# Hybrid attention and S5 block: PSUM copies moved to ScalarE, and three stretches reordered

## The chip, the core and the metric

The kernel runs on one core of a Trainium2 chip. The metric is the time of one execution on the device in microseconds (us). The engines are called PE (TensorE, matrix products and transposes, results in PSUM), DVE (VectorE), ACT (ScalarE), POOL (GpSimd) and SP (SyncE, which issues most DMAs). PE, DVE and ACT each work through a queue of their own in order, and wait on semaphores for one another.

## What is computed

One layer of a decoder trunk over 512 tokens of width 1024, all in float32. Two sub-layers, each with RMS norms and a modulation from a condition vector:

```python
h = rms_norm(x) * (1 + sc1) + sh1
z = h @ w_in                      # feeds three causal mixers
y_gla = gated_linear_attention(...)   # 4 heads; chunk state + in-chunk scores
y_ml  = mlstm(short_convolution(...)) # 4 heads
y_s5  = s5_state_space(...)           # 32 groups, complex diagonal states
merged = gate0*(y_gla@proj_gla) + gate1*(y_ml@proj_ml) + gate2*(y_s5@proj_s5)
x = x + (1 + gt1) * rms_norm(merged @ w_out)
h = rms_norm(x) * (1 + sc2) + sh2
x = x + (1 + gt2) * rms_norm((silu(h@w_gate) * (h@w_up)) @ w_down)
```

## The kernel before

**Products in three passes.** To get float32 accuracy, each operand of a large product is split into a high and a low half (`split`, line 234): ACT casts the high half (line 229), DVE subtracts to get the low half (line 220). A product is then three matmuls (`passes`, line 421: high by high, high by low, low by high). So each weight tile of 128x1024 costs ACT one cast and DVE one subtraction, and PE's pass with the low half waits for DVE.

**Who fixes the order.** In most of the kernel the instructions are written in program order and a planner sorts each engine's queue by its own idea of costs and priorities; the trace shows the sorted order, with later work often ahead of earlier work. The start (`head`) and the stretch from the output projection to the first part of the feed-forward network (`region`, from line 1627) are under `manual_schedule`: there PE, DVE and ACT follow the written order.

**Fillers.** Large projections of h (the gates, the attention's values, the S5 inputs and so on) are jobs that `fill(n)` and `FL.until(...)` place between the steps of the mixers, so that PE has products to do while DVE and ACT work on a mixer. Each job ends with a function that takes the result out of PSUM: `ev_conv` (first step of the short convolution), `ev_su` (S5 input, written in reversed order), `ev_gv` and others.

**Attention (lines 910 to 1206).** After the first projection sweep, q, k and the decay logits are copied out of PSUM (`qT`, `kT`, `ga`, `ii`, `lf`), a log-sigmoid chain on ACT gives the decays, `level` builds the scores `ST` (DVE-heavy, 14 calls), `kdT` holds the transposed decayed keys. Then, for each pair of heads `p`, the states `Sg` of the first three tiles of 128 tokens follow one another. After that comes, tile by tile, the output `og[t]`: tile 0 needs no state, tiles 1 to 3 need that of the tile before. Each output is scaled by the diagonal and squared for the norm; `rstd` is a chain of twelve small DVE steps; then 16 scalings by the norm and the gate `gr` (tile by tile, inside it head by head), and `to_fm` transposes 16 blocks of 128x128, four to a head, from which head by head the halves for the next product are made. PSUM banks for all these small products come from a pool of four (`ax_bank`).

**S5 (lines 1210 to 1331).** `params(b)` builds tables by outer products on DVE (`outer`), with a small product `ks` taken out of PSUM; `states(b)` and `outputs(b)` follow.

**Output projection (lines 1584 to 1683).** `half(t, h)` is the projection of token tile t, half h of the columns (24 matmuls). `gated`, `normed`, `x1_out`, `second` are the norms and the residual on ACT and DVE, the last giving `xn`; `to_h2(t)` transposes `xn` (8 transposes) and splits the result into `h2`. `S.ahead(ffn0_i[j], 0)` makes the halves of a weight tile, hi(j) and lo(j). `slab0(t)` is the first slab of the feed-forward product of tile t (24 matmuls, two k-steps to a weight tile).

Of the kernel before, what the change touches and what calls it, by code (L numbers as in the profile page):

```python
# [8 lines left out]
AF = mybir.ActivationFunctionType  # L9
OP = mybir.AluOpType  # L10
# [174 lines left out]
def _emit(tc, nc, ctx, ExitStack, A, out, act, dve, pool, pe, sp):  # L185
# [23 lines left out]
    def slot(name="s", dt=F32, tag="s"):  # L209
        return pools[tag].tile([128, 512], dt, tag=tag, name=name)  # L210
# [4 lines left out]
    def ax_bank(name="ax"):  # L215
        return axp.tile([128, 512], F32, tag="ax", name=name)
# [5 lines left out]
    def ts(e, o, a, s1, s2, op0, op1=OP.bypass):  # L222
        e.tensor_scalar(out=o, in0=a, scalar1=s1, scalar2=s2, op0=op0, op1=op1)

    def stt(o, a, s, b, op0, op1):
        dve.scalar_tensor_tensor(out=o, in0=a, scalar=s, in1=b, op0=op0, op1=op1)  # L226
# [4 lines left out]
    def cp(o, i, e=dve):  # L231
        e.tensor_copy(out=o, in_=i)
# [12 lines left out]
    def P(name, i=None, n=1, rows=slice(0, 128)):  # L245
        o, w = _PV[name]
        return pv[rows, o:o + w] if i is None else pv[rows, o + i:o + i + n]
# [107 lines left out]
    S = Stream()  # L355
# [296 lines left out]
    def ev_conv(f):  # L652
        def e(ps):
            u = slot("conv", tag="v")
            w = lambda j: P("conv_w", f * 4 + j)
            ts(dve, u, ps, w(3), P("conv_b", f), OP.mult, OP.add)
            for j in range(3):
                d = 3 - j
                stt(u[:, d:512], ps[:, 0:512 - d], w(j), u[:, d:512], OP.mult, OP.add)
            af(u, u, AF.Silu)  # L660
            conv[f] = u
        return e
# [3 lines left out]
    def ev_su(f):  # L666
        def e(ps):
            u = slot("su")
            cp(u.rearrange("p (a n) -> p a n", a=8)[:, ::-1], ps.rearrange("p (n a) -> p a n", a=8))
            sp.dma_start(out=su_d[f].rearrange("a p n -> p a n"), in_=u.rearrange("p (a n) -> p a n", a=8))  # L670
            U[f] = upool.tile([128, 512], F32, tag="U", name="U")
            sp.dma_start(out=U[f], in_=su_d[f].rearrange("a (c g) n -> (a c) (g n)", g=8))
        return e
# [242 lines left out]
    for p in range(2):  # L916
        qT[p], kT[p] = slot("gq"), slot("gk")
        af(qT[p], sweep_ps[p], AF.Copy, scale=0.125)
        cp(kT[p], sweep_ps[2 + p])
    ts(dve, ii[0:4], ii[0:4], P("i_b", rows=slice(0, 4)), None, OP.add)  # L920
    fill(1)
    cum = {}
# [208 lines left out]
    for p in range(2):  # L1131
        cv = cum[p].rearrange("p (t i) -> p t i", t=4)
        kd = slot("kd")
        kdv = kd.rearrange("p (t i) -> p t i", t=4)
        tt(dve, kdv[:, 0:3], cv[:, 0:3, 127:128].broadcast_to([128, 3, 128]), cv[:, 0:3], OP.subtract)
        af(kd[:, 0:384], kd[:, 0:384], AF.Exp, scale=1.0 / 16)
        tt(dve, kd[:, 0:384], kd[:, 0:384], kT[p][:, 0:384], OP.mult)
        ecum[p] = slot("ecum", tag="y")
        af(ecum[p], cum[p], AF.Exp, scale=1.0 / 16)
        qE[p] = slot("qE", tag="y")  # L1140
        tt(dve, qE[p], ecum[p], qT[p], OP.mult)
        ps = ax_bank()
        for t in range(3):
            pe.transpose(out=ps[:, t * 128:(t + 1) * 128], in_=kd[:, t * 128:(t + 1) * 128], identity=ident)
        kdT[p] = slot("kdT", tag="y")
        cp(kdT[p][:, 0:384], ps[:, 0:384])
    FL.until("gv")
    fill(2)
    for p in range(2):
        Sg[p] = slot("Sg", tag="y")  # L1150
        for t in range(3):
            ps = ax_bank()
            mm(ps[:, 0:256], lhsT=kdT[p][:, t * 128:(t + 1) * 128], rhs=gv[t][:, p * 256:(p + 1) * 256],
               start=True, stop=True)
            for h in range(2):
                r = slice(64 * h, 64 * h + 64)
                o = Sg[p][r, t * 128:(t + 1) * 128]
                if t == 0:
                    cp(o, ps[r, h * 128:(h + 1) * 128])
                else:  # L1160
                    stt(o, Sg[p][r, (t - 1) * 128:t * 128], ecum[p][r, t * 128 + 127:t * 128 + 128],
                        ps[r, h * 128:(h + 1) * 128], OP.mult, OP.add)
        fill(1)
    og = {}
    ssg, rg = st3[:, 16:32], st3[:, 32:48]
    for t in range(4):
        ps = [ax_bank(), ax_bank()]

        for h in range(4 if t else 0):
            p, hh = h // 2, h % 2  # L1170
            r = slice(64 * hh, 64 * hh + 64)
            mm(ps[hh][:, p * 128:(p + 1) * 128], lhsT=qE[p][r, t * 128:(t + 1) * 128],
               rhs=Sg[p][r, (t - 1) * 128:t * 128], start=(p == 0), stop=False)
        for h in range(4):
            p, hh = h // 2, h % 2
            a = (t % 2) * 2 + hh
            mm(ps[hh][:, p * 128:(p + 1) * 128], lhsT=ST[p, t // 2][:, a * 128:(a + 1) * 128],
               rhs=gv[t][:, h * 128:(h + 1) * 128], start=(t == 0 and p == 0), stop=(p == 1))
        og[t] = slot("og")
        for h in range(4):  # L1180
            sl = slice(h * 128, (h + 1) * 128)
            stt(og[t][:, sl], gv[t][:, sl], dg[:, t * 4 + h:t * 4 + h + 1],
                ps[h % 2][:, (h // 2) * 128:(h // 2 + 1) * 128], OP.mult, OP.add)
            junk = slot("junk")
            af(junk[:, 0:128], og[t][:, sl], AF.Square, accum_out=ssg[:, t * 4 + h:t * 4 + h + 1])
        fill(1)
    rstd(rg, ssg, 16, 128.0)
    FL.until("gr")
    for t in range(4):
        for h in range(4):  # L1190
            sl = slice(h * 128, (h + 1) * 128)
            stt(og[t][:, sl], og[t][:, sl], rg[:, t * 4 + h:t * 4 + h + 1], gr[t][:, sl], OP.mult, OP.mult)
    fill(5)
# [43 lines left out]
    def params(b):  # L1237
        pr = slice(4 * b, 4 * b + 4)
        CA[b] = big("CA")
        outer(CA[b], s5c[:, 0], s5c[:, 1], 0, pr, -1)  # L1240
        wp = big("wp")
        outer(wp, bb[:, 0], bb[:, 1], 1, pr, 1)
        bs = slot("bs")
        bv = bs[:, 0:256].rearrange("p (g c) -> p g c", c=32)
        pool.memset(bs[:, 0:256], 0.0)
        b2 = bv[:, :, 0:16].rearrange("p (a g) c -> p a g c", g=2)
        for g, r, q in ((0, even, odd), (1, odd, even)):
            cp(b2[r, :, g], bb[r, 0, pr])
            cp(b2[q, :, g], bb[r, 1, pr])
        fill(1)  # L1250
        kp = ax_bank()
        for g in range(8):
            q = (g % 4) * 32
            mm(kp[q:q + 32, (g // 4) * 128:(g // 4 + 1) * 128], lhsT=bv[:, g], rhs=CA[b][:, g * 128:(g + 1) * 128],
               start=True, stop=True, tile_position=(0, q))
        ks = slot("ks")
        cp(ks[:, 0:256], kp[:, 0:256])
        for j in range(2):
            stt(ks[:, j * 128:j * 128 + 16], C("dmask"), P("s5_d", 2 * b + j), ks[:, j * 128:j * 128 + 16],
                OP.mult, OP.add)  # L1260
        for q in range(4):
            sp.dma_start(out=kd_d.rearrange("(j q) c x -> q c j x", q=4)[q, :, 2 * b:2 * b + 2, 128:256],
                          in_=ks[q * 32:q * 32 + 16, 0:256].rearrange("p (j x) -> p j x", j=2))
        WT[b] = big("WT")
        for h in range(2):
            ps = ax_bank()
            for g in range(4):
                o = (h * 4 + g) * 128
                pe.transpose(out=ps[:, g * 128:(g + 1) * 128], in_=wp[:, o:o + 128], identity=ident)
            (lambda o, i: af(o, i, AF.Copy))(WT[b][:, h * 512:(h + 1) * 512], ps)  # L1270
        Mt[b] = big("M")
        for a in range(8):
            sp.dma_start(out=Mt[b][a * 16:(a + 1) * 16].rearrange("p (g x) -> p g x", g=8),
                         in_=kd_d[8 * b:8 * b + 8, :, 16 + 16 * a:144 + 16 * a].rearrange("g c x -> c g x"))
        fill(2)
# [278 lines left out]
    def normed(t):  # L1554

        r = root_inv(col(t))
        for h in range(2):
            stt(yg[t][h], yg[t][h], r, xre[t][h], OP.mult, OP.add)
# [80 lines left out]
    gated(2, yp, wslot)  # L1639
    S.ahead(ffn0_i[0], 0)  # L1640
    half(3, 0)
    normed(2)
    to_h2(0)
    S.ahead(ffn0_i[1], 0)
    x1_out(2)
    S.ahead(ffn0_i[2], 0)
    to_h2(1)
    S.ahead(ffn0_i[3], 0)
    half(3, 1)
    second(2)  # L1650
    x_tile(3, wslot, A["x"], sp)
    gated(3, yp, wslot)
    slab0(0)
    to_h2(2)
    normed(3)
    x1_out(3)
    slab0(1)
    second(3)
    slab0(2, range(4))
    slab0_g(0)  # L1660
# [85 lines left out]
```

## Time and profile before

| | |
|---|---|
| median of 3 runs | 912.28 us (910.48 to 912.75) |
| the profiled execution | 910.4 us, span of its instructions 908.6 us |
| PE busy in the span | 98% |
| DVE busy | 63% |
| ACT busy | 36% |
| mean granted TensorE clock | 0.989 |

A row of a timeline gives the start from the beginning of the span, the duration, the engine, the line, the operation, the program's names (output<-inputs), the shapes and how many instructions are merged into it; in brackets stands how long the engine sat idle before it and what ended that. L220, L226, L229 and L232 are helpers (`tt`, `stt`, `af`, `cp`), so names tell more than lines. Durations overlap a little: the distance from one start to the next is what an instruction costs its engine. The profile models the end of a matmul, so PE reads as busy when its matmuls follow closely, whatever paces them.

### The profile page before, as it was taken

Reading aid. Unit: us, or ns where it says so; the run is one execution under the profiler, and the core shown is the slowest. Engines: PE = TensorE matmul, PEld = TensorE weight load, DVE = VectorE, ACT = ScalarE, POOL = GpSimd, SP = SyncE. Lnnn points to the kernel's source line nnn. Section 1 sums busy time; section 2 is a strip of 40 time slices with the busy share of each in tenths; the row PEclk is TensorE's granted clock in tenths of the full one; section 3 lists DMA queues with packets and bytes.
Section 4 is the critical chain, followed back from the end, with each engine's and each line's share of the span. In section 5 each row is a group of like instructions: output and inputs, shape, how many; then the busy total and the mean of one; then the engine's idle time right before and its main releaser. Section 6 shows DMA issues by size and latency. Waiting matters only on the chain.

```text
span 908.6 us, 11582 instructions
## 1 busy us (share of the span) xinstructions
PE 888.7 (98%) x4334; PEld 723.1 (80%) x4334; DVE 575.7 (63%) x1144; ACT 331.0 (36%) x512; POOL 24.9 (3%) x68
## 2 busy tenths in 40 slices
PE   9999999999989999999999989999999999999997
PEld 7667887878878878788888868888888888888885
DVE  6748999979879884966679497544433333322215
ACT  4339323431442462722334444333222332211113
POOL 2010000000000000010000000000000000000000
PEclk7999999999999999999999999999999999999999
DMA  9661341233443442345456533533333323322303
GB/s 364 251 193 47 116 128 58 82 125 111 154 139 108 121 116 93 131 127 172 153 175 226 199 140 117 185 116 117 118 126 130 113 93 116 115 93 97 113 1 139
DMA packets 52193, 120.79 MB, mean 133 GB/s; under 512 B 13797, under 2 KB 19429, under 8 KB 52137
## 3 DMA queue, kind: packets, MB, share of 16 engines
q1 hardware_dynamic: 49944, 115.92, 38.0%
q0 software_dynamic: 1040, 2.38, 1.1%
q10 hardware_dynamic: 1152, 1.75, 0.5%
q8 instruction: 34, 0.56, 0.3%
q14 instruction: 23, 0.18, 0.1%
HBM read 113.21 MB, written 6.82 MB: 132 GB/s over the span
## 4 chain that ended last, share of the span: by engine, by line
PE 77%; DVE 17%; issue 2%; ACT 2%; DMA 1%; SPq 0%; DVEq 0%; ACTq 0%
PE mm L422 16%; PE mm L423 16%; PE mm L424 16%; PE y L1527 5%; PE y L1526 5%; PE y L1528 5%; DVE lo L220 3%; PE mm L455 2%; PE mm L454 2%; PE mm L456 2%; DVE ST L1111 1%; DVE Qp L220 1%; DVE o L220 1%; DVE D L220 1%; PE ax L1318 1%
## 5 line engine op out<-in xcount | busy, mean ns | idle before, releaser
L229 ACT ACTIVATE hi<-raw 128x1024 fp32r<-128x1024 f32 (+2 forms) x157 | 151.9, 971 | 382.2 <-PE mm L423 156.2
L220 DVE TENSOR_TENSOR lo<-raw,hi 128x1024 fp32r<-128x1024 f32 (+2 forms) x157 | 174.6, 1114 | 155.6 <-ACT hi L229 155.0
L424 PE MATMUL mm<-h2hi,lo 128*128 128x512 f32 x320 | 124.6, 389 | 0.0
L423 PE MATMUL mm<-h2lo,hi 128*128 128x512 f32 x320 | 124.6, 389 | 0.0
L422 PE MATMUL mm<-h2hi,hi 128*128 128x512 f32 x320 | 124.5, 389 | 0.0
L424 PE MATMUL mm<-hT,lo 128*128 128x512 f32 x280 | 110.7, 395 | 3.1 <-DVE lo L220 3.1
L422 PE MATMUL mm<-hT,hi 128*128 128x512 f32 x280 | 112.3, 401 | 0.2 <-ACT hT L229 0.2
L423 PE MATMUL mm<-hT,hi 128*128 128x512 f32 x280 | 111.0, 396 | 0.4 <-DVE hT L226 0.4
L422 PEld LDWEIGHTS mm<-h2hi,hi 128*128 128x128 f32 x320 | 60.1, 188 | 12.5
L424 PEld LDWEIGHTS mm<-h2hi,lo 128*128 128x128 f32 x320 | 60.1, 188 | 12.4
L423 PEld LDWEIGHTS mm<-h2lo,hi 128*128 128x128 f32 x320 | 60.1, 188 | 12.3
L1528 PE MATMUL y<-hi,g 128*128 128x512 f32 x176 | 68.5, 389 | 0.0
L1527 PE MATMUL y<-lo,g 128*128 128x512 f32 x176 | 68.5, 389 | 0.0
L1526 PE MATMUL y<-hi,g 128*128 128x512 f32 x176 | 68.3, 389 | 0.0
L220 DVE TENSOR_TENSOR sg<-sg,mm 128x512 f32<-128x512 f32 x36 | 24.7, 685 | 64.8 <-PE mm L424 64.7
L422 PEld LDWEIGHTS mm<-hT,hi 128*128 128x128 f32 x280 | 53.2, 190 | 15.7 <-issue 4.0
L424 PEld LDWEIGHTS mm<-hT,lo 128*128 128x128 f32 x280 | 53.2, 190 | 14.6 <-DVE lo L220 3.5
L423 PEld LDWEIGHTS mm<-hT,hi 128*128 128x128 f32 x280 | 53.1, 190 | 11.9 <-DVE hT L226 1.2
L226 DVE SCALAR_TENSOR_TENSOR gacc<-raw,cact,gacc 128x512 f32<-128x512 f32 x56 | 41.9, 748 | 21.9 <-DMA raw<-ada 21.3
L455 PE MATMUL mm<-lo,hT 128*128 128x512 f32 x128 | 50.5, 394 | 0.4 <-DVE lo L220 0.4
L454 PE MATMUL mm<-hi,hT 128*128 128x512 f32 x128 | 49.8, 399 | 0.0
L456 PE MATMUL mm<-hi,hT 128*128 128x512 f32 x128 | 49.7, 391 | 0.0
(311 smaller groups left out, 1393.9 us busy)
## 6 DMA issues: line engine op xcount, KB each, us to landing
raw<-ada SPq DMA_DIRECT2D x48, 512.0 KB, 3.5
raw<-ffn SPq DMA_DIRECT2D x44, 512.0 KB, 3.3
raw<-wzg SPq DMA_DIRECT2D x24, 512.0 KB, 3.2
raw<-ffo SPq DMA_DIRECT2D x22, 512.0 KB, 3.3
raw<-wpr SPq DMA_DIRECT2D x24, 256.0 KB, 2.7
raw<-wout SPq DMA_DIRECT2D x8, 512.0 KB, 4.3
raw<-sweep SPq DMA_DIRECT2D x8, 384.0 KB, 8.5
xT<-xT SPq DMA_DIRECT2D x4, 512.0 KB, 5.6
```

Source lines behind the costliest of these rows:

```text
L220: e.tensor_tensor(out=o, in0=a, in1=b, op=op)
L226: dve.scalar_tensor_tensor(out=o, in0=a, scalar=s, in1=b, op0=op0, op1=op1)
L229: act.activation(out=o, in_=i, func=f, **kw)
L422: mm(ps, lhsT=whi, rhs=xhi, start=first, stop=False)
L423: mm(ps, lhsT=whi, rhs=xlo, start=False, stop=False)
L424: mm(ps, lhsT=wlo, rhs=xhi, start=False, stop=last)
L454: mm(ps[t], lhsT=xh[:, tk], rhs=hi[:, sl], start=(k == 0), stop=False)
L455: mm(ps[t], lhsT=xh[:, tk], rhs=lo[:, sl], start=False, stop=False)
L456: mm(ps[t], lhsT=xl[:, tk], rhs=hi[:, sl], start=False, stop=(k == 7))
L1526: mm(ps, lhsT=xhi, rhs=whi[:, sl], start=first, stop=False)
L1527: mm(ps, lhsT=xhi, rhs=wlo[:, sl], start=False, stop=False)
L1528: mm(ps, lhsT=xlo, rhs=whi[:, sl], start=False, stop=last)
```

## The change

Sixteen copies or first steps out of PSUM move from DVE (`cp`, `ts`) to ACT (`af`): the first step of the convolution, the S5 input, `kT`, `kdT` and `ks`. In the attention, the body of the output loop becomes `gla_out(t)`; tile 0's outputs are written ahead of the states, and the 16 scalings go head by head, inside that tile by tile. In the output projection, `half(3, 1)` moves between the two transposes of tiles 0 and 1, the second norm of tile 2 moves behind the gating of tile 3, and tile 2's transposes move behind tile 3's norm and between the halves of `slab0(1)`.

```diff
-            ts(dve, u, ps, w(3), P("conv_b", f), OP.mult, OP.add)
+            af(u, ps, AF.Identity, scale=w(3), bias=P("conv_b", f))
...
-            cp(u.rearrange("p (a n) -> p a n", a=8)[:, ::-1], ps.rearrange("p (n a) -> p a n", a=8))
+            af(u.rearrange("p (a n) -> p a n", a=8)[:, ::-1], ps.rearrange("p (n a) -> p a n", a=8), AF.Copy)
...
-        cp(kT[p], sweep_ps[2 + p])
+        af(kT[p], sweep_ps[2 + p], AF.Copy)
...
-        cp(kdT[p][:, 0:384], ps[:, 0:384])
+        af(kdT[p][:, 0:384], ps[:, 0:384], AF.Copy)
     FL.until("gv")
     fill(2)
-    for p in range(2):
-        Sg[p] = slot("Sg", tag="y")
...
     og = {}
     ssg, rg = st3[:, 16:32], st3[:, 32:48]
-    for t in range(4):
+    def gla_out(t):
         ps = [ax_bank(), ax_bank()]
...
         fill(1)
+
+    gla_out(0)
+    for p in range(2):
+        Sg[p] = slot("Sg", tag="y")
...
+        fill(1)
+    for t in range(1, 4):
+        gla_out(t)
     rstd(rg, ssg, 16, 128.0)
     FL.until("gr")
-    for t in range(4):
-        for h in range(4):
+    for h in range(4):
+        for t in range(4):
             sl = slice(h * 128, (h + 1) * 128)
             stt(og[t][:, sl], og[t][:, sl], rg[:, t * 4 + h:t * 4 + h + 1], gr[t][:, sl], OP.mult, OP.mult)
...
-        cp(ks[:, 0:256], kp[:, 0:256])
+        af(ks[:, 0:256], kp[:, 0:256], AF.Copy)
...
     half(3, 0)
-    normed(2)
     to_h2(0)
     S.ahead(ffn0_i[1], 0)
+    half(3, 1)
+    normed(2)
+    S.ahead(ffn0_i[2], 0)
     x1_out(2)
-    S.ahead(ffn0_i[2], 0)
+    S.ahead(ffn0_i[3], 0)
     to_h2(1)
-    S.ahead(ffn0_i[3], 0)
-    half(3, 1)
-    second(2)
     x_tile(3, wslot, A["x"], sp)
     gated(3, yp, wslot)
+    second(2)
     slab0(0)
-    to_h2(2)
     normed(3)
     x1_out(3)
-    slab0(1)
+    slab0(1, range(4))
+    to_h2(2)
+    slab0(1, range(4, 8))
     second(3)
```

## Rows read from the trace of the kernel before

**Rows 1.** The page, part 1: busy us, share of the span, instructions of each engine.

```profile
PE 888.7 (98%) x4334; PEld 723.1 (80%) x4334; DVE 575.7 (63%) x1144; ACT 331.0 (36%) x512; POOL 24.9 (3%) x68
```

**Rows 2.** The waits of PE: engine, line, releaser: us in total, times, longest.

```profile
PE mm L424 <- DVE lo L220: 3.1, 1, 3.1
PE ax L1580 <- DVE xn L220: 1.9, 3, 0.7
PE ax L1200 <- DVE og L226: 1.6, 1, 1.6
...
PE ax L1177 <- DVE Sg L226: 1.1, 1, 1.1
```

**Rows 3.** Windows: stretch, length, busy us of PE, PEld, DVE, ACT, POOL, clock, DMA.

```profile
66.00:77.00 11.00, 10.93 (x45) 7.75 (x44) 8.20 (x13) 8.89 (x10) 0.00 (x0) 1.00 0.18 51
77.00:160.00 83.00, 81.31 (x440) 68.34 (x438) 81.59 (x228) 34.92 (x54) 0.00 (x0) 1.00 0.28 89
...
168.00:190.00 22.00, 20.36 (x88) 15.76 (x86) 21.68 (x50) 5.88 (x11) 0.31 (x1) 0.92 0.25 83
190.00:233.00 43.00, 43.00 (x293) 35.67 (x292) 35.12 (x60) 15.36 (x26) 1.49 (x5) 1.00 0.44 138
...
525.90:554.15 28.25, 24.18 (x118) 18.77 (x116) 25.36 (x55) 14.13 (x29) 1.03 (x2) 1.00 0.32 113
```

**Rows 4.** Timeline of PE at 185 us: start, us, instruction, idle before.

```profile
185.35 4.32 PE L1200 MATMUL ax<-ident,og 128*128 128x128 f32 x16 [1.64 <-DVE og L226]
```

**Rows 5.** Timeline of DVE, 166 to 189 us.

```profile
166.86 0.46 DVE L223 TENSOR_SCALAR st<-st 128x16 f32<-128x16 f32 x3 [1.00 <-ACT junk L229]
...
184.95 4.28 DVE L226 SCALAR_TENSOR_TENSOR og<-og,st,gr 128x128 f32<-128x128 f32 x16
```

**Rows 6.** Timeline of PE, 525 to 555 us.

```profile
525.88 1.03 PE L1580 MATMUL ax<-ident,xn 128*128 128x128 f32 x8
...
554.15 0.48 PE L1608 MATMUL ax<-hi,h2hi 128*128 128x512 f32 x1
```

**Rows 7.** Timeline of DVE, 68 to 140 us.

```profile
68.79 1.28 DVE L232 COPY gk<-mm 128x512 f32<-128x512 f32 x2
...
72.60 0.69 DVE L220 TENSOR_TENSOR g<-g,t 128x512 f32<-128x512 f32 x1 [1.49 <-ACT t L229]
...
108.20 0.68 DVE L232 COPY su<-mm 128x512 f32<-128x512 f32 x1
108.80 0.76 DVE L1111 COPY_PREDICATED ST<-gm,ax 128x256 f32<-128x256 int32 x2
...
138.32 0.55 DVE L232 COPY kdT<-ax 128x384 f32<-128x384 f32 x1
138.79 0.18 DVE L220 TENSOR_TENSOR x<-ph,w 128x32 f32<-128x32 f32 x1
```

**Rows 8.** Timeline of ACT, 63 to 95 us.

```profile
63.24 1.30 ACT L229 ACTIVATE gq<-mm 128x512 f32<-128x512 f32 x2 [2.97 <-PE mm L424]
67.99 0.69 ACT L229 ACTIVATE t<-ax,pv 128x512 f32<-128x512 f32 x1 [3.46 <-PE ax L935]
...
90.79 0.58 ACT L229 ACTIVATE gv<-mm 128x512 f32<-128x512 f32 x1
94.00 1.31 ACT L229 ACTIVATE D<-D 128x512 f32<-128x512 f32 x2 [2.63 <-DVE D L220]
```

**Rows 9.** Timeline of DVE, 528 to 538 us.

```profile
528.64 0.21 DVE L223 TENSOR_SCALAR st<-st 128x1 f32<-128x1 f32 x2
...
537.13 1.23 DVE L220 TENSOR_TENSOR lo<-raw,hi 128x1024 fp32r<-128x1024 f32 x1 [0.99 <-ACT hi L229]
```

**Rows 10.** Timeline of ACT at 548 us.

```profile
548.13 0.63 ACT L229 ACTIVATE junk<-yg 128x512 f32<-128x512 f32 x1 [2.60 <-issue]
```

**Rows 11.** Timelines of DVE at 233 us and of PE at 255 us.

```profile
233.28 0.69 DVE L220 TENSOR_TENSOR x<-ax,ph 128x512 f32<-128x512 f32 x1 [2.47 <-PE ax L1283]
...
255.62 0.50 PE L424 MATMUL mm<-hT,lo 128*128 128x512 f32 x1 [3.08 <-DVE lo L220]
```

More of the change, by code (lines that the diff above doesn't have):

```diff
@@ L1145, in _emit @@
         kdT[p] = slot("kdT", tag="y")
-        cp(kdT[p][:, 0:384], ps[:, 0:384])
+        af(kdT[p][:, 0:384], ps[:, 0:384], AF.Copy)
     FL.until("gv")
     fill(2)
-    for p in range(2):
-        Sg[p] = slot("Sg", tag="y")
[L1151 to L1163, printed above, removed]
     og = {}
     ssg, rg = st3[:, 16:32], st3[:, 32:48]
-    for t in range(4):
+    def gla_out(t):
         ps = [ax_bank(), ax_bank()]
@@ L1186, in _emit @@
         fill(1)
+    gla_out(0)
+    for p in range(2):
+        Sg[p] = slot("Sg", tag="y")
+        for t in range(3):
+            ps = ax_bank()
+            mm(ps[:, 0:256], lhsT=kdT[p][:, t * 128:(t + 1) * 128], rhs=gv[t][:, p * 256:(p + 1) * 256],
+               start=True, stop=True)
+            for h in range(2):
+                r = slice(64 * h, 64 * h + 64)
+                o = Sg[p][r, t * 128:(t + 1) * 128]
+                if t == 0:
+                    cp(o, ps[r, h * 128:(h + 1) * 128])
+                else:
+                    stt(o, Sg[p][r, (t - 1) * 128:t * 128], ecum[p][r, t * 128 + 127:t * 128 + 128],
+                        ps[r, h * 128:(h + 1) * 128], OP.mult, OP.add)
+        fill(1)
+    for t in range(1, 4):
+        gla_out(t)
     rstd(rg, ssg, 16, 128.0)
     FL.until("gr")
-    for t in range(4):
-        for h in range(4):
+    for h in range(4):
+        for t in range(4):
             sl = slice(h * 128, (h + 1) * 128)
```

## Prediction

> **What bounds the kernel now.** I read the busy line of the page first, then what TensorE (PE) waits for, then the busy time by stretch, then the timelines around each wait. PE is busy for 98% of the span, VectorE (DVE) for 63%, ScalarE (ACT) for 36% [rows 1]. PE's work is not changed by this edit (the same matmuls in another order), so it can win or lose only what PE idles, or spends in matmuls paced by someone else. The PE waits are few: 3.1 us for the low half of a weight split, 1.9 us and more around the transposes of the output projection, 1.6 us before the transposes of the attention output, 1.1 us for a state of the attention [rows 2]. All releasers are DVE. The stretches say why: from 77 to 160 us DVE is busy 81.59 of 83.00 us, from 168 to 190 us 21.68 of 22.00, while ACT is busy for 34.92 of 83 and 5.88 of 22 [rows 3]. There DVE is the true clock, and PE keeps up because its queue holds projection products; where these run out it waits. In 190 to 233 us PE has no gap at all (43.00 of 43.00), so less DVE work there is worth nothing.
>
> The largest single loss is at the end of the attention. PE waits 1.64 us, then does 16 transposes in 4.32 us [rows 4]; DVE does the 16 scalings that feed them in 4.28 us [rows 5], so the transposes go at DVE's pace of 0.27 us. Eight transposes whose inputs mostly lay ready took 1.03 us, 0.13 each [rows 6]; 16 are worth 2.06, so 1.64 + 4.32 - 2.06 = 3.9 us of PE time are lost there.
>
> **The change, part by part.** *PSUM copies to ACT.* Sixteen DVE operations go (two of kT, four of su, two of kdT, four of the short convolution, four of ks); only those in DVE-bound stretches count.
> - su 1 to 3 (three alike): the copy starts at 108.20 and the next instruction at 108.80, so 0.60 each, 1.80 in all. kdT (two alike): 138.32 to 138.79, 0.47 each, 0.94 in all [rows 7]. Together 2.74 us, all between 77 and 160 us, ahead of the attention's scalings: -2.74.
> - kT (two in 1.28 us) and su 0, at 68 to 70 us: DVE waits soon after for ACT (1.49 us at 72.60) [rows 7], so the 1.8 us freed only lengthen that wait: 0. On ACT the three fit into the 3.46 us it idles before 67.99 [rows 8], as their banks are the sweep's and fill before that. If they are queued behind that point instead, all that follows is late by 3 x 0.58 = 1.74 (below).
> - The convolution's first step and ks (256 columns, so under the 0.55 us of kdT) run behind 190 us, where PE has no wait that they end [rows 2, 3]: 0.
> - Price on ACT: a PSUM copy of 512 columns takes 0.58 (gv), and one with a bias column 0.69 [rows 8]. The reversed order in which su is written, and the convolution's second operand column, don't show on ACT; bounds are 0.58 and twice that, 1.16. I take 0.69, as DVE shows no surcharge for su's order (0.68 with it, 1.28 for kT's two without). With ACT busy 42% of 77 to 160 us, either end is covered. What is queued behind such a copy on ACT are the high halves of weight splits; at ACT's load they come up to 1 us later, and the DVE half behind them waits in a queue that is itself late. The next work of ACT behind the gv copy is an Exp, and no table load stands between [rows 8], so the copies don't switch tables.
>
> The rows say that a PSUM copy costs ACT what it costs DVE (0.58 against 0.60). The Trainium skill ("ScalarE: Activation LUTs", Rules for kernel authors) says the contrary for plain arithmetic: use VectorE, not ScalarE. Its formula (same page, What ACT_TABLE_LOAD costs) makes a copy of 512 columns 186 + 0.833 x 512 = 613 ns and the convolution's step, with two operand columns, 799 ns, both estimates; by it the sum is the same as long as ACT has idle time.
>
> *First tile's outputs ahead of the states.* Tile 0 needs no state, and its matmuls waited 1.05 of the 1.1 us for a bank held by state work [rows 2]. Alone this is no gain: DVE does the same work in another order, and PE, arriving earlier, waits longer at the scalings. But DVE itself waits 1.00 us for the last squares on ACT before it can start the root [rows 5]; with tile 0's four squares done early, up to 1.0 of it goes. Bounds 0 and 1.0; I take 0.5, as the last tile's squares stay last: -0.5.
>
> *Scaling head by head.* The 16 scalings keep their 4.28 us, and the last transpose still follows the last scaling, so nothing on DVE. What changes: head 0 is complete after 4 scalings, not 13, so its split and the first product from it can be queued between heads. If PE's queue takes products there, the time lost to the pace, 4.32 - 2.06 = 2.26 us, is filled; if not, 0. The order is a planner's and the trace of before doesn't show it. I take the middle, as the products stood ready (PE ran without a gap right after) yet none had been put between the 16: -1.1.
>
> *Output projection.* Here PE, DVE and ACT follow the written order, so I walked both orders through with the durations of the trace. Walking the old order gives the start of PE's second half of slab 2 at 554.2 us; the trace has 554.15 [rows 6]. DVE starts tile 2's gating at 528.64 [rows 9] and has the same list to finish until tile 3's second norm in both orders. PE now fills with half(3,1) before the second pair of transposes, so its waits of 0.47 and 0.73 go; slab 0 starts at 533.0 instead of 534.8. But it needs lo(2) and lo(3), and DVE's wait of 0.99 for a high half [rows 9] comes back one split later: hi(3) stands on ACT behind the root of tile 2's second norm, whose input DVE makes behind lo(2). And h2's split of tile 2 now stands behind tile 3's norm and its two squares of 0.63 [rows 10] on ACT and DVE; the walk gives a new DVE wait of 0.7 and a PE wait of 1.2 before slab 2, against 0.2 on DVE that go. Result: 554.7, so +0.5. Bounds: DVE idles 28.25 - 25.36 = 2.9 us of this stretch [rows 3], of which I see at most 1.2 to gain; the loss can be 1.2.
>
> *Sum.* -2.74 - 0.5 - 1.1 + 0.5 = -3.84 us. Up to 190 us it asks 4.34 of the 1.05 + 3.9 = 4.95 us that PE loses there, so there is room. The 3.08 us at 255.62 stay: that burst starts when DVE gets the S5 states' matmuls (2.47 us of waiting at 233.28) [rows 11], so it moves along with PE. The profiled execution took 910.4 (span 908.6); 910.4 - 3.84 = 906.6. The median of the three runs, 912.28, is 1.9 above it, so I forecast **908.4**.
>
> **Rivals.**
> 1. *More than the sum.* The planner, with DVE lighter, puts the weight split of 255.62 ahead of the outer products, and the 3.08 us go too: about 905.3. For: 3 us are there, and DVE spends the last of them on outer products, which could wait. Against: nothing edited lies between 233 and 256.
> 2. *No change.* DVE's freed 2.74 us are filled with work of the S5 parameters, which already stood between the root's small steps (166.86 to 184.95 [rows 5]); the scalings start no earlier, and the tail costs 0.5: 912.28 - 0 to 1.6 + 0.5, about 912. For: the root's twelve steps, 0.15 us each by the first three, took 18 us. Against: that work needs the S5 tables, of which there is a fixed amount.
> 3. *ACT becomes late.* The three copies at 63 to 70 us go behind the log-sigmoid chain; ACT is busy 8.89 of 11.00 us there [rows 3]. The DVE-bound stretch starts 1.74 us later: -3.84 + 1.74 = -2.1, so 910.2. [...] Against: the copies' inputs are ready first.
> 4. *Slower.* A changed order puts another weight split behind a DVE burst, as at 255.62; PE's queue is in order, so it costs up to 3.08, and with the tail's 0.5 and no gain elsewhere 915.9. With no gain it decides once such waits pass 2.2 us; with the gains intact only past 6.5. Against: DVE has less work before each split than now.
>
> **How the numbers follow.** About 0.3%, 2.7 us, is what a measurement can tell from no change. Forecast (gain of 2.7 to 5.5) 0.42, rival 1 (5.5 to 9) 0.16, rival 2 0.22, rival 3 0.08, rival 4 0.12. So faster 0.58, same 0.30, slower 0.12. The likeliest's own range is 906.8 to 909.6. To hold 8 in 10 the range goes from 903.5 (within rival 1) to 912.5 (rivals 2 and 3 whole): outside stay rival 4 and a twentieth for the rest.
>
> **What would show it.** Right: no wait before the first tile's matmuls near 148 us; PE idle plus pace at the 16 transposes down from 3.9 us to about 1; DVE rows of su, kdT gone from 108 to 140 us; products between the transposes of different heads; from tile 2's gating on DVE to the second half of slab 2 on PE 26.0 us instead of 25.5, with a PE wait of about a microsecond before slab 2; 3.1 us at about 252 still there. Wrong: the S5 outer products moving further ahead of the scalings (rival 2), copies of kT behind a table load (rival 3), or a new PE wait on a low half (rival 4).

## The result, and the profile after

The changed kernel takes 919.2 us (median of 4 runs, 917.99 to 920.95), the kernel before beside it 911.38: a ratio of 1.0091, with a 95% interval from 1.0069 to 1.0114. It is about 8 us slower, where 908.4 was forecast. The profiled execution took 918.0 us, with a span of 916.2.

The page's busy line of the changed kernel:

```profile
PE 889.7 (97%) x4334; PEld 723.3 (79%) x4334; DVE 567.3 (62%) x1128; ACT 337.0 (37%) x526; POOL 24.9 (3%) x68
```

DVE does 8.4 us less than in [rows 1] and ACT 6.0 us more (the sixteen copies take it 9.0 us, and two table loads of 1.28 us are gone). PE's work is the same, so the loss is time in which PE idles or runs slowly. What PE waits for in the changed kernel (columns as in [rows 2]):

```profile
PE mm L424 <- DVE lo L220: 5.0, 1, 5.0
PE ax L1204 <- DVE og L226: 4.6, 1, 4.6
...
PE mm L455 <- DVE lo L220: 1.2, 1, 1.2
PE ax L1322 <- DMA ys_d<-Y: 1.1, 1, 1.1
```

The two waits that the forecast wanted to shorten or leave alone have grown: the one for the low half of a weight split from 3.1 to 5.0 us, the one ahead of the transposes of the attention output (line 1200 before, 1204 now) from 1.6 to 4.6. The 1.1 us for a state [rows 2] are gone, as predicted. The 1.2 us at line 455, 0.4 before, are for a weight's low half at 87 us. The windows of the same stretches as [rows 3], and of the two stretches around the grown waits:

```profile
66.00:77.00 11.00, 11.00 (x47) 8.47 (x46) 5.26 (x9) 10.87 (x15) 0.00 (x0) 1.00 0.19 50
77.00:160.00 83.00, 81.53 (x437) 68.67 (x435) 81.51 (x228) 38.47 (x60) 0.00 (x0) 1.00 0.28 89
168.00:190.00 22.00, 17.42 (x74) 13.86 (x73) 21.51 (x54) 5.25 (x8) 0.31 (x1) 0.90 0.31 102
...
185.50:192.30 6.80, 5.63 (x17) 4.30 (x18) 6.77 (x21) 1.19 (x2) 0.00 (x0) 0.50 0.34 111
254.50:264.10 9.60, 4.63 (x12) 3.58 (x12) 9.30 (x19) 0.00 (x0) 0.00 (x0) 0.64 0.32 103
```

From 66 to 77 us ACT is now busy for 10.87 of 11 us (8.89 before) and DVE for only 5.26 (8.20). From 77 to 160 us DVE is as full as before, 81.51 us, although 2.7 us of copies have left it. Around both waits PE's granted clock falls to 0.50, the lower of its two levels, for a while (the 0.64 of the second window is a mean of both levels). PE's timeline shows what that costs:

```profile
186.67 2.31 PE L1204 MATMUL ax<-ident,og 128*128 128x128 f32 x8 [4.58 <-DVE og L226]
188.63 0.78 PE L422 MATMUL mm<-yhi,hi 128*128 128x512 f32 x1
189.21 0.63 PE L422 MATMUL mm<-hT,hi 128*128 128x512 f32 x1
189.63 0.63 PE L423 MATMUL mm<-hT,hi 128*128 128x512 f32 x1
...
192.73 0.40 PE L422 MATMUL mm<-hT,hi 128*128 128x512 f32 x1
192.96 0.39 PE L423 MATMUL mm<-hT,hi 128*128 128x512 f32 x1
...
194.57 1.04 PE L1204 MATMUL ax<-ident,og 128*128 128x128 f32 x8
...
235.03 1.20 PE L1287 MATMUL ax<-U,WT 128*64 128x64 f32 x32
...
259.55 0.79 PE L424 MATMUL mm<-hT,lo 128*128 128x512 f32 x1 [4.97 <-DVE lo L220]
260.14 0.63 PE L422 MATMUL mm<-hT,hi 128*128 128x512 f32 x1
260.56 0.63 PE L423 MATMUL mm<-hT,hi 128*128 128x512 f32 x1
...
556.93 0.50 PE L1612 MATMUL ax<-hi,h2hi 128*128 128x512 f32 x1 [0.81 <-DVE h2lo L220]
...
561.70 0.48 PE L1612 MATMUL ax<-hi,h2hi 128*128 128x512 f32 x1
```

Behind each long wait a product of 512 columns takes 0.42 us from start to start (189.21 to 189.63). At full clock it takes 0.23 (192.73 to 192.96). Eight transposes are now done, then products, then the other eight: the products between the heads did come. The tail behaves as the walk through the written order said: tile 2's gating to the second half of slab 2 takes 535.72 (below) to 561.70, 25.98 us, with a PE wait of 0.81 before slab 2. DVE's timeline of the changed kernel:

```profile
72.11 0.69 DVE L220 TENSOR_TENSOR g<-g,t 128x512 f32<-128x512 f32 x1 [3.14 <-ACT t L229]
...
186.26 4.29 DVE L226 SCALAR_TENSOR_TENSOR og<-og,st,gr 128x128 f32<-128x128 f32 x16
...
236.93 0.69 DVE L220 TENSOR_TENSOR merged<-sg,mm 128x512 f32<-128x512 f32 x1 [4.68 <-PE mm L424]
237.53 0.74 DVE L226 SCALAR_TENSOR_TENSOR gacc<-raw,cact,row 128x512 f32<-128x512 f32 x1
238.19 0.68 DVE L220 TENSOR_TENSOR x<-ax,ph 128x512 f32<-128x512 f32 x1
...
535.72 0.21 DVE L223 TENSOR_SCALAR st<-st 128x1 f32<-128x1 f32 x2
```

Three things are to be seen. At 72 us DVE waits 3.14 us for ACT instead of 1.49 [rows 7]. The scalings start at 186.26 instead of 184.95 [rows 5], although PE's decay product (line 935) came 1.68 us earlier in this execution (65.09 against 66.77); counted from it they start 3.0 us later. And the S5 state step (`x<-ax,ph`) starts 1.96 us after its products on PE have ended (235.03 + 1.20 = 236.23), behind `merged` and a `gacc`; before it started at 233.28 [rows 11], 0.04 us after their end at 233.24. The wait for the low half that hangs on this chain grew by the same 1.9 us (3.08 to 4.97).

ACT's timeline shows the first of these:

```profile
65.06 0.60 ACT L229 ACTIVATE su<-ax 128x512 f32<-128x512 f32 x1 [5.78 <-PE ax L424]
...
66.98 0.63 ACT L229 ACTIVATE gk<-mm 128x512 f32<-128x512 f32 x1
67.46 0.73 ACT L229 ACTIVATE t<-ax,pv 128x512 f32<-128x512 f32 x1
```

ACT idles 5.78 us and then does five copies in one go. The first in the queue is su, whose bank fills last: `ev_su(0)` is written ahead of the loop that copies q and k. Both copies of gq, which ran at 63.24 before [rows 8], now stand behind it. The log-sigmoid chain (`t`) starts 2.37 us after its product at 65.09; before it was 67.99 - 66.77 = 1.22.

### The profile page after: what moved, and what is told of

It reads as the page before. It is cut to its first block, busy times and chain, and to the rows that moved or that the text cites. A ratio compares the mean times of both kernels' runs of the same rounds, so it can differ in the third digit from the quotient of the medians.

```text
span 916.2 us, 11587 instructions
## 1 busy us (share of the span) xinstructions
PE 889.7 (97%) x4334; PEld 723.3 (79%) x4334; DVE 567.3 (62%) x1128; ACT 337.0 (37%) x526; POOL 24.9 (3%) x68
## 4 chain that ended last, share of the span: by engine, by line
PE 66%; DVE 14%; DMA 3%; issue 2%; ACT 1%; SPq 1%; DVEq 0%; ACTq 0%
PE mm L422 13%; PE mm L424 13%; PE mm L423 13%; PE y L1531 5%; PE y L1530 5%; PE y L1532 5%; DVE lo L220 2%; DVE o L220 2%; PE mm L456 2%; PE mm L455 2%; PE mm L454 2%; DMA kd_d<-ks 1%; DVE wp L220 1%; DVE y L220 1%; DVE xn L226 1%
```

## The experiments

Each ratio is to the kernel before on the same chip, from 5 to 12 runs of the experiment. 0.1% is 0.9 us.

| kernel | ratio | 95% interval | us |
|---|---|---|---|
| e1: sixteen copies | 1.0057 | 1.0040 to 1.0074 | +5.2 |
| e2: first tile | 1.0059 | 1.0041 to 1.0076 | +5.4 |
| e3: heads | 0.9992 | 0.9978 to 1.0006 | -0.7 |
| e4: output projection | 0.9997 | 0.9988 to 1.0007 | -0.3 |
| e5: ks | 1.0035 | 1.0020 to 1.0050 | +3.2 |
| e6: the other twelve copies | 1.0023 | 1.0011 to 1.0036 | +2.1 |
| e7: first tile, heads | 1.0071 | 1.0057 to 1.0086 | +6.5 |
| e8: e6, heads, output projection | 1.0023 | 1.0010 to 1.0036 | +2.1 |
| e9: kT, first su | 1.0027 | 1.0015 to 1.0038 | +2.5 |
| e10: su 1 to 3, kdT, convolution | 0.9993 | 0.9981 to 1.0004 | -0.6 |
| e11: e7, its products behind the states | 1.0075 | 1.0062 to 1.0088 | +6.8 |
| e12: low half last | 1.0012 | 1.0001 to 1.0022 | +1.1 |
| e13: e7, phase table late | 0.9989 | 0.9980 to 0.9998 | -1.0 |
| e14: e10, heads, output projection, phase table late | 0.9983 | 0.9974 to 0.9992 | -1.5 |
| e15: e14 and first tile | 0.9972 | 0.9960 to 0.9983 | -2.6 |
| e16: phase table late alone | 1.0003 | 0.9993 to 1.0014 | +0.3 |
| e17: the change, ks on DVE | 1.0087 | 1.0073 to 1.0100 | +7.9 |
| e18: the change, phase table late | 1.0014 | 1.0001 to 1.0026 | +1.3 |

### The four parts by themselves (e1 to e4)

Each is the kernel before with one part of the change.

e1 has the sixteen copies:

```diff
-            ts(dve, u, ps, w(3), P("conv_b", f), OP.mult, OP.add)
+            af(u, ps, AF.Identity, scale=w(3), bias=P("conv_b", f))
...
-        cp(kT[p], sweep_ps[2 + p])
+        af(kT[p], sweep_ps[2 + p], AF.Copy)
...
```

e2 has the first tile ahead, e3 the scalings head by head:

```diff
+    gla_out(0)
     for p in range(2):
         Sg[p] = slot("Sg", tag="y")
...
+    for t in range(1, 4):
+        gla_out(t)
```

```diff
-    for t in range(4):
-        for h in range(4):
+    for h in range(4):
+        for t in range(4):
```

e4 has the output projection as in the change:

```diff
     half(3, 0)
-    normed(2)
     to_h2(0)
     S.ahead(ffn0_i[1], 0)
+    half(3, 1)
+    normed(2)
...
```

> Only the sixteen PSUM copies on ScalarE; the order of attention and output projection as before. Theory 1 (the reordering of the attention loses the time, the copies don't): 909 to 912, the log-sigmoid chain starts about 1.2 us later but DVE's 2.7 us make up for it; PE's wait for the first scaling about 1 us, its wait for the low half of the split at 255 us still 3.1. Theory 2 (the copies lose it: ScalarE late at 65 us, and with other queue orders behind): 915 to 919, PE's wait for the low half at 255 to 260 us grows to about 5.

> Only the first tile's outputs ahead of the states. Theory 1: 914 to 918; other DVE work takes the place of the states, which come some 4 us later than in the kernel before (145.5 us), the first scaling comes later than 185, and PE's wait ahead of the transposes grows from 1.64 to 4 us or more, with half the clock behind it. Theory 2: 911 to 913, states and scalings within 1 us of before.

> Only the 16 scalings head by head. My prediction's step: products go between the heads' transposes, up to 2.26 us gained, so 909 to 911. Rival: the planner leaves the 16 transposes together, or the pace of the scalings turns into a wait: 911 to 912.

> Only the reordered output projection. The walk through the written order gave +0.5, and the changed kernel's trace shows +0.3 for this stretch: 911.5 to 912. Rival: the stretch does better with the kernel before's clock in front of it, or worse by up to 1.2: 910.2 to 912.6.

Neither theory of e1 and e2 is right alone: the copies cost 5.2 us and the first tile 5.4. The heads and the output projection cost nothing that can be measured. Theory 1 (the copies don't lose time) falls.

### Which copies (e5, e6, e9, e10)

e5 has the four copies of ks alone, e6 the other twelve. e9 has kT and the su copy of quarter 0 alone, e10 the su copies of quarters 1 to 3, kdT and the convolution. The diffs of e5 and, for su, of e10:

```diff
-        cp(ks[:, 0:256], kp[:, 0:256])
+        af(ks[:, 0:256], kp[:, 0:256], AF.Copy)
```

```diff
-            cp(u.rearrange("p (a n) -> p a n", a=8)[:, ::-1], ps.rearrange("p (n a) -> p a n", a=8))
+            if f:
+                af(u.rearrange("p (a n) -> p a n", a=8)[:, ::-1], ps.rearrange("p (n a) -> p a n", a=8), AF.Copy)
+            else:
+                cp(u.rearrange("p (a n) -> p a n", a=8)[:, ::-1], ps.rearrange("p (n a) -> p a n", a=8))
```

> Only the four copies of ks (256 columns each, 0.4 us) on ScalarE, which my prediction priced at nothing. Order theory (the edits cost nothing where they stand; the planner, whose order shifts with any edit, puts a weight's low half behind DVE's S5 burst): DVE's queue now has the sixth low half of the S5 stretch behind Xs, o and wp as in the kernel with all copies, so 914 to 917, with PE waiting 2 to 3 us for it near 222 us and some 2 us near 260, where the kernel before waits 3.1 at 252. Engine-time theory (copies on ScalarE cost what ScalarE loses): 911 to 912, as ScalarE has idle time there.

> The other twelve copies on ScalarE (convolution, su, kT, kdT), ks left on DVE. Order theory: DVE's queue behind 195 us stands as in the kernel before, so no new wait there; 910 to 913, the log-sigmoid chain about 1 us late against 2.7 us that DVE saves. Engine-time theory: 915 to 917, as with all sixteen, because the copies at 65 us and of su and kdT make the loss.

> Only the three copies at 63 to 70 us on ScalarE (kT twice, su of the first quarter). DVE's order behind 195 us is that of the kernel before. My prediction's step (they fit into ScalarE's idle time): no change, 911 to 912. My third rival (they go behind or ahead of the log-sigmoid chain and make it late by up to 1.74 us): PE's wait near 87 us 1.1 instead of 0.4, first scaling 0.5 to 1.7 later, 912 to 913.5.

> The other nine copies (su of quarters 1 to 3, kdT, convolution) on ScalarE; kT, the first su and ks on DVE. Order behind 195 us nearly that of the kernel before. My prediction's step (DVE's 2.7 us go through to the scalings): 908.5 to 909.5, first scaling at about 182.2 instead of 185. My second rival (DVE's freed time is filled with S5 parameter work and waiting): first scaling within 0.7 us of 185, 911 to 912.

**ks.** Four copies of 0.4 us cost 3.2 us. Up to 195 us the trace is that of the kernel before to 0.1 us. Then DVE's order differs. The kernel before has:

```profile
218.28 1.22 DVE L220 TENSOR_TENSOR lo<-raw,hi 128x1024 fp32r<-128x1024 f32 x1
219.41 1.70 DVE L220 TENSOR_TENSOR Xs<-x,y 64x252 f32<-64x252 f32 x4
```

and e5 (first DVE, then PE):

```profile
217.78 1.70 DVE L220 TENSOR_TENSOR Xs<-x,y 64x252 f32<-64x252 f32 x4
219.51 0.69 DVE L220 TENSOR_TENSOR o<-pw,bb 128x512 f32<-128x512 f32 x1
220.12 1.38 DVE L220 TENSOR_TENSOR wp<-o,o 64x512 f32<-64x512 f32 x2
221.53 0.75 DVE L226 SCALAR_TENSOR_TENSOR gacc<-raw,cact,gacc 128x512 f32<-128x512 f32 x1
222.20 1.22 DVE L220 TENSOR_TENSOR lo<-raw,hi 128x1024 fp32r<-128x1024 f32 x1
```

```profile
223.47 0.80 PE L424 MATMUL mm<-hT,lo 128*128 128x512 f32 x1 [2.69 <-DVE lo L220]
224.06 0.63 PE L422 MATMUL mm<-hT,hi 128*128 128x512 f32 x1
```

In the kernel before that low half ran at 218.28, ahead of Xs, o and wp. Here it runs behind them, 3.9 us later, and PE waits 2.69 us and then goes on at half clock. The 3.08 us near 255 are gone; 1.09 us (for `bs`) and 0.62 us (for a low half) stand there instead. So these waits make 4.40 us, only 1.3 more than before, and 13 products of 512 columns at half clock add 2.6 us; the profile of the kernel before has no such product between 60 and 910 us. Nothing in the four copies takes that time: the planner drew another order. The same order stands in e1 and e2, with waits of 2.69 and 1.83 us at the same place.

**kT and the first su** cost 2.5 us, more than either expectation. e9's trace shows ACT's burst of the changed kernel and the same 3.14 us on DVE; PE's wait at 87 us is 1.15 us instead of 0.38, and the scalings start 1.3 us later, counted from the decay product. But PE idles only 0.6 us more than in the kernel before (11.1 against 10.5 between 60 and 910 us), while 14 products at half clock, behind its waits at 185 and 257 us, take 2.8 us. Most of this execution's loss is in the granted clock, and that the late ACT brings it is not shown. My third rival (1.74 us) was near in size, not in path: the copies don't stand behind the log-sigmoid chain but ahead of it.

**su 1 to 3, kdT and the convolution** give 0.6 us, within the interval of nothing. The scalings start at 182.36:

```profile
182.36 4.28 DVE L226 SCALAR_TENSOR_TENSOR og<-og,st,gr 128x128 f32<-128x128 f32 x16
```

That is 2.59 us earlier than before, but this execution's decay product came 1.86 us earlier, so 0.73 are left of DVE's 2.74. In e6, which has kT and the first su as well, DVE works 4.0 us less between the decay product and the scalings and idles 5.5 us more (11.1 instead of 5.6); the scalings start 1.5 us later. What it saves, it waits. At 914.3 e6 is slower than the order theory allowed.

### Combinations (e7, e8) and the order of PE's products (e11, e12)

e7 is e2 and e3 together; e8 is e6 with the heads and the output projection. e11 is e7 with the block of projection products that `gla_out(0)` issues behind the states, e12 the kernel before with the branch projections' products in another order:

```diff
-        fill(1)
+        if t:
+            fill(1)
...
+    fill(1)
     for t in range(1, 4):
         gla_out(t)
```

```diff
                 for k in range(4):
-                    o = k * 128
-                    passes(ps, hi[:, o:o + 128], lo[:, o:o + 128], *yb["y", b][k], k == 0, k == 3)
+                    for z in range(2):
+                        mm(ps, lhsT=hi[:, k * 128:k * 128 + 128], rhs=yb["y", b][k][z], start=(k + z == 0), stop=False)
+                for k in range(4):
+                    mm(ps, lhsT=lo[:, k * 128:k * 128 + 128], rhs=yb["y", b][k][0], start=False, stop=(k == 3))
```

> First tile ahead and scaling head by head, no copies moved, output projection as before. Behind 195 us DVE's queue has the low half ahead of Xs, o and wp again, other than with the first tile alone. Order theory: the wait near 224 us (1.8 with half the clock behind it) goes, the 4.8 us ahead of the transposes stay, the wait near 254 grows past 3.1: 913 to 916. If the first tile costs its time at the scalings alone, and not through the order: 916 to 917 less 0.7 for the heads, so about 916.

> The change without its two suspects: twelve copies (not ks), heads and output projection, states ahead of the first tile as before. Order theory: 909 to 912, the order behind 195 us as in the kernel before. Engine-time theory: 915 to 917.

> As the run with the first tile ahead and the scaling head by head, but the block of projection products that the first tile's function issues after itself stands behind the states again. If those twelve products ahead of the states on PE make the states late: first scaling from 4.1 us later than before to about 1 to 2, PE's wait ahead of the transposes from 4.8 to 2 to 3, 913 to 915.5. If not (the first tile's banks or DVE's order do it): 917 to 918 as without it.

> The kernel before, with the products of the branch projections in another order: the eight with the high half of the weight first, the four with the low half last, so that the low half may come 6 products, 1.4 us, later. If a low half that is late behind DVE's S5 burst is what PE waits for there, the 3.07 us near 252 become 1.7 or less: 908.5 to 910.5. If the planner's order shifts with this edit too, a wait elsewhere takes its place: 911 to 914.

e7's order behind 195 us is the kernel before's again up to the state step, so the wait at 224 goes; yet it costs 6.5 us (917.7, above both ranges expected), with the two grown waits of the changed kernel (4.82 and 4.97). Order alone behind 195 us doesn't explain the first tile. e8 costs what the twelve copies cost (913.7, between its two ranges).

e11 rules out the twelve products that the first tile issues ahead of the states. The first products of the states (`ax<-gv,kdT`) start on PE 2.8 us earlier than in e7, and DVE still takes the first state out at the same time. First e7 (its first state, 149.87, stands below), then e11:

```profile
143.39 1.02 PE L1178 MATMUL ax<-gv,kdT 128*128 128x256 f32 x4
```

```profile
140.58 1.03 PE L1179 MATMUL ax<-gv,kdT 128*128 128x256 f32 x4
149.76 0.60 DVE L232 COPY Sg<-ax 64x128 f32<-64x128 f32 x2
```

So the states' inputs lie ready for 5 us and more, and it is DVE's queue that makes the states late. e12 is inconclusive as a remedy: the wait at 252 falls from 3.08 to 0.99 + 0.62 and 0.92 some 9 us earlier, but the order shifts and 1.5 us of waiting appear at 488 us.

### The phase table (e13 to e16)

DVE's queue in e7 has work of the S5 phase table (`ph`, doubled step by step) in front of the states. The edit queues the last two doublings, 6.5 us of DVE, behind the last state `Sg` (`issue_after` fixes the order in DVE's queue alone). It is written behind the loop of the states. e13 is e7 with it; e14 is e10 with heads, output projection and it; e15 adds the first tile to e14; e16 has it alone:

```diff
         for m in (1, 2, 4, 8, 16, 32):
+            if m == 16:
+                yield 'late'
+                xs5, ys5 = slot('x5'), slot('y5')
...
-    for _ in prm:
-        pass
+    for z in prm:
+        if z == 'late':
+            break
...
+    with tc.issue_after(last_sg.ins):
+        for z in prm:
+            pass
```

> As the run with the first tile ahead and the scaling head by head, but the last two doublings of S5's phase table (products of 256 and 512 columns on DVE, 6.5 us in all) are queued on DVE behind the attention's last state. If the first tile ahead costs its time because DVE then has table work in front of the states and nothing left to fill its waits at the end of the attention: states start at 145 us or earlier instead of 150, first scaling within 1 us of 185 instead of 189, DVE's queue behind 195 us is that of the kernel before, 909.5 to 912.5. If the first tile's PSUM banks or PE's order make the states late: states still at 148 or later, 915 to 918.

> Candidate for better than both: the nine copies that did no harm (su of quarters 1 to 3, kdT, convolution), heads, output projection, phase table late, states ahead of the first tile as before. If the table work was what took DVE's 2.7 us: first scaling at 181 to 183 instead of 185, 908 to 910. If the chain to the scalings is bound by PE's products and ScalarE: first scaling at 184 to 185, 910 to 911.5.

> The same with the first tile ahead of the states: all of the change but the copies of ks, kT and the first su, with the phase table late. If the first tile ahead is worth something once DVE's order lets the states through: first scaling earlier than in the run with the states ahead, 907.5 to 910. If its place is worth nothing either way: within 0.7 us of that run.

> The kernel before with the phase table late alone, as the control. If that order costs the kernel before time at 135 to 150 us: first scaling 1 to 2.5 us earlier than 185, 909 to 911. If not: 911 to 912.5, as the table work only moves behind the states and DVE idles as much in front of the root.

This decides it. DVE in e7, from the first tile's outputs to the root:

```profile
144.26 0.86 DVE L226 SCALAR_TENSOR_TENSOR og<-gv,st,ax 128x128 f32<-128x128 f32 x3
...
146.67 0.42 DVE L220 TENSOR_TENSOR y<-ph,w 128x256 f32<-128x256 f32 x1
...
149.44 0.42 DVE L220 TENSOR_TENSOR ph<-ph,y 128x256 f32<-128x256 f32 x1
...
149.87 0.60 DVE L232 COPY Sg<-ax 64x128 f32<-64x128 f32 x2
...
164.36 1.12 DVE L226 SCALAR_TENSOR_TENSOR og<-gv,st,ax 128x128 f32<-128x128 f32 x4 [0.35 <-PE ax L1162]
166.99 1.23 DVE L220 TENSOR_TENSOR lo<-raw,hi 128x1024 fp32r<-128x1024 f32 x1 [1.51 <-ACT hi L229]
168.75 1.12 DVE L226 SCALAR_TENSOR_TENSOR og<-gv,st,ax 128x128 f32<-128x128 f32 x4 [0.53 <-PE ax L1162]
170.73 0.46 DVE L223 TENSOR_SCALAR st<-st 128x16 f32<-128x16 f32 x3 [0.86 <-ACT junk L229]
```

and in e13:

```profile
143.96 0.85 DVE L226 SCALAR_TENSOR_TENSOR og<-gv,st,ax 128x128 f32<-128x128 f32 x3
...
146.36 0.60 DVE L232 COPY Sg<-ax 64x128 f32<-64x128 f32 x2
...
154.69 0.42 DVE L220 TENSOR_TENSOR x<-ph,w 128x256 f32<-128x256 f32 x1
...
166.62 0.46 DVE L223 TENSOR_SCALAR st<-st 128x16 f32<-128x16 f32 x3 [0.86 <-ACT junk L229]
```

In e7 the first state comes at 149.87, 5.6 us after the first tile's outputs; the table's doubling of 256 columns (146.67 to 149.78) stands between. Then nothing is left to fill DVE while the outputs of tiles 1 to 3 come in, and it idles four times ahead of the root. In e13 the first state comes 3.5 us earlier, the table work fills the waits, and the root starts 4.1 us earlier. The order behind 195 us is the kernel before's, the wait at 252 is 3.07 again, and 7.5 us are gone: 0.9989 instead of 1.0071. The states came a little later (146.36) than the 145 that I had expected. The edit does two things, states earlier and work left for the waits; their shares were not separated.

e16, the control, is no faster than the kernel before, so the late table is worth something with the first tile ahead. With DVE lighter no gain in time is shown: e14's 1.5 us are no more than what e10, the heads and the output projection (0.6, 0.7 and 0.3) make without it. e14 starts the scalings at 181.95, e15 at 181.63. With the late table the first tile ahead is worth 1.0 us more, with intervals that overlap. e13, e14 and e15 all beat the kernel before, with intervals below 1; **e15 is the fastest**: 908.0 us, by the ratios 2.6 us faster than the kernel before and 11 faster than the change as made.

### What the change owes to ks (e17, e18)

e17 is the change with ks on DVE, e18 the whole change with the phase table late as above. The diff of e17 against the changed kernel:

```diff
-        af(ks[:, 0:256], kp[:, 0:256], AF.Copy)
+        cp(ks[:, 0:256], kp[:, 0:256])
```

> The whole change with ks alone put back on DVE. Its queues stand as the changed kernel's. Order theory: the four copies cost 3 us alone only because the order flips with them; here it doesn't, so 918 to 919.5, no gain. Engine-time theory (ks costs where it stands): 915 to 916.5.

> The whole change, all sixteen copies, with the phase table late. The first tile's loss should go (5 to 6 us) and the states come through; but with ks on ScalarE the queue behind 195 us again has the sixth low half behind Xs, o and wp, as with ks alone. Order theory: 911.5 to 914.5, PE waiting 2 to 3 us near 220 and some 2 near 256, and the log-sigmoid chain about 1 us late. If ks and the log-sigmoid chain cost nothing now: 907 to 909, as without those copies.

With ks back on DVE the change costs the same (1.0087 against 1.0091): its order is not flipped by ks, and no cost of ks can be seen in it (the two intervals leave room for some 2 us). In e18 the order is flipped, the first tile's loss is gone, and PE waits for three low halves, 3.6 us in all, the longest 2.7, as in e5. It stands 0.42% (3.8 us) above e15, which has kT, the first su and ks on DVE.

## Why the prediction was wrong

The forecast was faster (0.58); slower had 0.12. The cause is what rival 4 says in general, a queue order in which what PE waits for stands late on DVE, but through a step that I had given a gain. Its price was too low as well: rival 4's 915.9 has one wait of up to 3.08 us, while here two waits grew, by 2.9 and 1.9 us, with half clock behind both. Point by point:

- **First tile ahead: -0.5 forecast, +5.4 alone, +6.5 with the heads. This is the step that failed.** I wrote that DVE does the same work in another order and took bounds of 0 and -1.0, with no loss. But the states are the start of the chain to the scalings, and the first tile is work that needs no state. In front of the states it delays them, with the table work that the planner put beside it; behind them it had covered DVE's waits. e13 shows it: with the table behind the states the loss is gone; in the whole change (e18) the same edit takes the ratio from 1.0091 to 1.0014, 7 us. A second part of the price is the S5 state step behind `merged` (1.9 us of wait, in e7, e11, e17 and the changed kernel alike, always 4.97 instead of 3.07). These four have the first tile ahead, the heads and the table early; with the first tile alone (e2) the low halves are flipped instead, and with the heads alone (e3) or the table late (e13, e15) the wait is 3.07 or 3.08. That the order alone makes the 1.9 us is read from the trace, not tried.
- **The clock: no term.** I counted what PE idles and what it spends at another engine's pace. In the profile of the changed kernel PE idles 5.9 us more than before between 60 and 910 us (16.4 against 10.5), and 16 products of 512 columns behind the two grown waits run at half clock, 3.2 us more. The 16 transposes, with products between them, take 2.9 us instead of 4.3. Together that makes 7.7 us; the spans differ by 7.6.
- **su 1 to 3 and kdT: -2.74 forecast, -0.7 at the scalings and -0.6 in time.** My second rival: DVE's time went into table work and waiting. With the table behind the states the scalings came 2.7 us earlier (181.95 against 184.95, the decay product 0.28 earlier), which is the whole forecast; the time of e14, heads and output projection included, gained 1.5. What takes the rest was not settled; in e14's profile PE idles as long as before (10.3 against 10.5 us between 60 and 910), and 12 products run at half clock, 2.4 us.
- **kT and the first su: 0 forecast, +2.5 measured (e9).** I had counted ACT's idle 3.46 us before the log-sigmoid as room. It is room only if the copies are queued by when their banks fill; the queue put the last bank first. That this makes the 1.3 us at the scalings is read from the trace, as no run queued the copies otherwise; most of e9's loss is half clock, and why it falls there is open. The forecast named a price for late copies, 1.74, and gave it 0.08.
- **ks: 0.** No cost can be seen in the change (e17). Alone it costs 3.2 us by its order (e5), which no row of the kernel before shows.
- **The price on ACT: right.** The rows of the changed kernel have 0.58 to 0.60 for su, 0.49 for kdT, 0.38 for ks and 0.76 for the convolution's step, for 512, 384, 256 and 512 columns; none above the bounds. The order in which su is written costs nothing.
- **Heads: -1.1 forecast, -0.7 measured with an interval of -2.0 to +0.5.** The products do stand between the heads.
- **Output projection: +0.5 forecast, -0.3 measured, interval -1.1 to +0.6.** The stretch takes 25.98 us where the walk gave 26.0 (25.5 before, so the +0.3 in e4's expectation should be +0.5). Here, where the order is written by hand, the walk through it was a good forecast.
- **The wait of 3.08 us "stays": wrong in the change** (4.97). It is 3.07 or 3.08 in e3, e4, e6, e8, e9 and e10, and with the table late (e13 to e16) whether the first tile is ahead or not; in e1 and e5, where ks moves, shorter waits take its place.

The parts add up: the twelve copies (+2.1), first tile and heads (+6.5) and the output projection (-0.3) make 8.3 us, by their intervals uncertain by some 2 us; measured are 8.3 (0.91% of 911.4).

The Trainium skill ("ScalarE: Activation LUTs", Rules for kernel authors) gives plain arithmetic (add, mul and the like) to VectorE, not ScalarE. Of the moved operations that is the convolution's first step. No harm shows here: e10, which moves its four steps and five copies to ScalarE, measures 0.9993 (0.9981 to 1.0004).

## What to carry to other kernels

Where a planner sorts the queues, an edit's price is the price of the order that it draws: before summing durations, see which instruction each long wait of TensorE hangs on, and compare what stands ahead of it in the two queues. In this kernel, work that needs nothing of a chain was best queued behind the chain's start, where it covers the chain's waits; and time freed on an engine is a gain only if the planner does not fill it with something else ready; here one edge that put table work behind the states turned a loss of 6.5 us into a gain of 1. A copy moved to an idle engine should be queued by when its input is ready: one that waits for the last bank holds up all behind it (read from the traces of e9 and the change; no run tried another order). And a wait of TensorE can cost more than its length, as the next section shows.

## What the runs showed of the hardware

The same wait of PE, 3.07 or 3.08 us for the same low half, leaves the granted clock at 1.00 in the profiled execution of the kernel before and takes it to half in that of e6. The windows of 12 us around the wait, first of the kernel before, then of e6 (columns as in [rows 3]):

```profile
252.00:264.00 12.00, 8.92 (x68) 7.24 (x66) 10.04 (x17) 2.03 (x3) 0.00 (x0) 1.00 0.50 174
```

```profile
253.50:265.50 12.00, 8.93 (x43) 6.55 (x42) 9.93 (x17) 1.06 (x1) 0.00 (x0) 0.72 0.49 175
```

PE is busy equally long, but starts 43 instructions instead of 68. In e6 thirteen products of 512 columns behind the wait take 0.43 us each instead of 0.23, 2.6 us in all. Eleven kernels have this wait of 3.07 or 3.08 us. Over the 12 us from its start the granted clock stayed at 1.00 in the profiled executions of three (the kernel before, e4, e13) and was 0.72 or 0.86 in eight (e3, e6, e8, e9, e10, e14, e15, e16).

The runs of one kernel differ in the same way: e6's twelve fall into two groups, three of 910.2 to 911.4 us with a mean granted clock of 0.993 to 0.995 and nine of 914.1 to 915.0 us with 0.986 to 0.989. That this wait is what parts the two groups is not shown, as each kernel was profiled once; but the granted clock does change from one execution of a kernel to the next, and part of a difference of 2 us in the table above can be how often it falls. The Trainium skill ("TensorE: Matmul & The Clock Gate", What's actually happening) says that the throttled state is the default and activity releases it; the trace agrees in that every half-clock stretch of these two executions between 60 and 900 us follows a wait of PE (1.64 us at 185 in the kernel before, 3.07 us at 257 in e6), and shows in addition that the same wait need not bring one.
